# A two-layer decoder trunk on one core: second-half operands formed later, six early units, and a second load queue

## The chip, the cores and the metric

The kernel runs on one core of one Trainium2 chip. The metric is device time in microseconds (us) of one execution, the median of several runs; lower is better. Engines are named as in the profile: PE (TensorE), DVE (VectorE), ACT (ScalarE), POOL (GpSimd) and SP (SyncE, which here issues transfers only; "SPq" is its queue).

## The reference

All is float32, with 1024 tokens and a model width of 1024. The change lies in the last four blocks:

```python
def _short_conv_layer(x, norm_w, in_w, conv_w, out_w):
    h = _rmsnorm(x, norm_w) @ in_w                     # 1024 -> 3 * 1024
    gate_b, gate_c, v = _split(h, (SC_WIDTH, SC_WIDTH, SC_WIDTH))
    y = gate_b * _causal_dwconv(gate_c * v, conv_w)
    return x + y @ out_w

def _swiglu_ffn(x, norm_w, w_gate, w_up, w_down):      # 1024 -> 2816 -> 1024
    h = _rmsnorm(x, norm_w)
    return x + (jax.nn.silu(h @ w_gate) * (h @ w_up)) @ w_down

# layer 0: x = attention and state-space mixer (x); x = _swiglu_ffn(x, ...)
# layer 1: x = _short_conv_layer(x, ...);           x = _swiglu_ffn(x, ...)
# then a last _rmsnorm
```

## The kernel before

The first 900 us (mixer layer) are not touched. From there the work is six matrix stages, each with a right and a left operand of 2 x 2 blocks: ffn0 in, ffn0 out, conv in, conv out, ffn1 in, ffn1 out. Every stage multiplies the blocks with seven products instead of eight (Strassen's scheme in Winograd's form), so sums of blocks are formed as operands. Float32 accuracy comes from a split into a high part (`hi`, a cast on ACT, L169) and a low part (`lo`, a subtraction on DVE, L170), and three matmuls: hi x hi, hi x lo, lo x hi.

An **in stage** (ffn0 in, conv in, ffn1 in) has x as right operand, normalised, as blocks H1 to H7 (`hh`, `hl`), and weights as left operand in units of 256 columns: 22 units for each ffn, 12 for the conv. A unit is seven products of 12 matmuls (`prod`, L1264 to L1266). Its raw weights come by two loads into the tag `wr` (L1215, two buffers), DVE forms four sums of them in place (product 6's step, L1226 to L1228, and product 3's), and each product's weights are split into a buffer `wc` (tag `w`, eight of them). Products 1 and 2 need only H1 and H2, which come from the first half of the tokens; the others need the second half. So the first `EARLY_U` = 4 units run their products 1 and 2 ahead ("early" products), while the second half is normalised, and these units have only five products later.

An **out stage** (ffn0 out, conv out, ffn1 out) runs its seven products one after the other, each over 11 k-steps (ffn) or 4 (conv). A k-step is again 12 matmuls (`step_on`, L1395 to L1397). Its left operand is loaded for two k-steps at once (`lr`, 512 KB, L1378, the same two buffers `wr`), its right operand for each (`rr`, 256 KB, L1380, tag `t` of 42 buffers). ACT and DVE split both into `wc` and `rh`, `rl`. The residual x is loaded from DRAM (L1565, in the last stage L1616), POOL adds an earlier product's result to it ahead of a product's steps (L1411 and L1414), DVE adds each product that comes (L1440), and `spill` (L1455) writes the new x back.

A **border** is the way from an out stage, or the mixer layer, to the next in stage. `norm_first` normalises the first half (L1468), `norm_second` the second: `rsbcast` yields the row factor `rb` (ACT L997, L998), then DVE normalises and forms the sums for H6, H7, H5, H4, H3 and splits all five (20 `lo` subtractions on L170).

`Steps(7)` prepares weights and operands up to seven steps ahead of PE (`self.st.get()`). All code is emitted by hand in this order; a scheduler then sorts the instructions by simulated time, and what comes out is one fixed list for each engine, run in order. Each DMA stands in the list of the engine that issues it, and a DMA that waits for its buffer holds up what stands behind it there. `wsums` (POOL) forms, beside an ffn's in stage, weight sums for the out stage and writes them to DRAM (`wd`, `d_wl`, L1329 and L1339).

Of the kernel before, what the change touches and what calls it, by code (L numbers as in the profile page):

```python
# [9 lines left out]
F32R = mybir.dt.float32r  # L10
# [65 lines left out]
class Steps:  # L76


    def __init__(self, ahead):
        self.ahead, self.fns, self.made, self.pos = ahead, [], [], 0  # L80

    def add(self, fn, test=None):
        self.fns.append((fn, test))

    def get(self):
        while len(self.made) < min(self.pos + self.ahead + 1, len(self.fns)):
            fn, test = self.fns[len(self.made)]
            if test is not None and not test():
                break
            self.made.append(fn())  # L90
        assert self.pos < len(self.made)
        r, self.made[self.pos] = self.made[self.pos], None
        self.pos += 1
        return r


class Trunk:
# [1105 lines left out]

    EARLY_U = 4

    def unit_steps(self, src, prods):

# [24 lines left out]

        for i in prods:
            self.st.add(lambda i=i: step(i))

# [13 lines left out]

    def plan_in(self, srcs):  # L1250

        for src in srcs[:self.EARLY_U]:
            self.early_steps(src)
        for n, src in enumerate(srcs):
            self.unit_steps(src, [i for i in self.UNIT if n >= self.EARLY_U or i not in (1, 2)])

# [112 lines left out]
    def plan_out(self, nk, order, L, R, ready):  # L1369

        nc = self.nc
        st = {}

        def step(i, k):
            if k % 2 == 0:
                n = min(2, nk - k)
                st["l"] = self.wp.tile([P, 2, HF], F32, name=self.uid("lr"), tag="wr", bufs=2)
                nc.sync.dma_start(st["l"][:, :n], L(i, k, n))  # L1378
            r = self.t(nm="rr")
            nc.sync.dma_start(r.rearrange("p (k m) -> p k m", k=1), R(i, k, 1))  # L1380
# [18 lines left out]
    def out_products(self, nk, order, load, done):  # L1399
# [4 lines left out]
        for n, i in enumerate(order):  # L1404
            for ab in {4: ((1, 0),), 2: ((0, 0),), 5: ((1, 1), (0, 1))}.get(i, ()):
                X[ab] = [load(ab, p) for p in range(4)]
            ps = [(self.ps, self.mm)[n % 2]() for _ in range(4)]
            pre = {4: ((1, 0), "u3"), 2: ((0, 0), "p1"), 5: ((1, 1), "u3")}.get(i)
            if pre:
                for p in range(4):  # L1410
                    self.add(X[pre[0]][p], X[pre[0]][p], U[pre[1]][p], nc.gpsimd)  # L1411
            if i == 5:
                for p in range(4):
                    self.add(X[0, 1][p], X[0, 1][p], U["u2"][p], nc.gpsimd)  # L1414
# [55 lines left out]

    def norm_second(self, key, H):

        nc = self.nc
        h0, h1 = self.HO
        x, w = self.x, [self.vt[key][:, k:k + 1] for k in range(KT)]
        rb = self.rsbcast(self.ssq[h1], 1.0 / D, self.last[h1])
        t3, t2 = [], []
        for k in range(4):
            t = self.s(nm="t3")
            nc.scalar.activation(t, x[k][h1], AF.Copy, scale=w[k])  # L1480
            nc.vector.scalar_tensor_tensor(t, x[4 + k][h1], w[4 + k], t, op0=ALU.mult, op1=ALU.subtract)
            t3.append(t)
        for k in range(4):
            nc.vector.tensor_tensor(t3[k], t3[k], rb, op=ALU.mult)
            t2.append(self.s(nm="t2"))
            self.add(t2[k], t3[k], x[k][h0])
            H.setdefault(6, []).append(self.hsplit(t2[k], self.t))
        H[7] = [self.hsplit(t, self.t) for t in t3]
        for k in range(4):
            b = x[k][h1]  # L1490
            nc.vector.scalar_tensor_tensor(b, b, w[k], rb, op0=ALU.mult, op1=ALU.mult)
            self.sub(b, b, x[k][h0])
            H.setdefault(5, []).append(self.hsplit(b, self.t))
        for k in range(4):
            b = x[4 + k][h0]
            self.sub(b, b, t2[k])
            H.setdefault(4, []).append(self.hsplit(b, self.s))
        for k in range(4):
            b = x[4 + k][h1]
            nc.vector.scalar_tensor_tensor(b, b, w[4 + k], rb, op0=ALU.mult, op1=ALU.mult)  # L1500
            H.setdefault(3, []).append(self.hsplit(b, self.s))


    def plan_ffn(self, ly, side):
# [4 lines left out]
        self.plan_in(srcs)  # L1509
        dn = a[ly + "_w_down"]  # L1510
# [50 lines left out]
    def xload(self, d):  # L1561
        def load(ab, p):
            j, hf = ab[0] * 4 + p, self.HO[ab[1]]
            t = self.s(nm="x")
            self.nc.sync.dma_start(t, d[j * P:(j + 1) * P, hf * HF:(hf + 1) * HF])  # L1565
            self.x[j][hf] = t
            return t
        return load

    def out_to_x(self, nk, d_x, d_new, key, H):  # L1570
# [3 lines left out]
        def done(ab, p, x):  # L1574
# [4 lines left out]
            if n[b] == KT:  # L1579
                if d_new is not None:  # L1580
                    self.spill(d_new, hf)
                else:
                    self.turn(hf)
# [18 lines left out]
    def out_final(self, st):  # L1602
# [37 lines left out]

    def plan_conv(self):
# [3 lines left out]
        self.plan_in(srcs)  # L1645
        dn = a["l1_out_w"]
# [12 lines left out]
    def conv_in(self, st, H, second):  # L1659
# [21 lines left out]

        def cb(q):
            def cons(i, j, t):
                o = S[q][1][i, j]
                nc.vector.tensor_tensor(o, t, o, op=ALU.mult)
            return cons
# [15 lines left out]
    def run(self):  # L1702
# [45 lines left out]
        self.st = Steps(7)  # L1748
        f0, cv, f1 = self.plan_ffn("l0", "R"), None, None
        cv = self.plan_conv()  # L1750
        f1 = self.plan_ffn("l1", "L")
        d = [self.dp.tile([D, T], F32, name=f"d_r{i}") for i in range(2)]
        self.d_xT = self.dp.tile([T, D], F32, name="d_xT")
        H = [{} for _ in range(3)]
        h0, h1 = self.HO
# [43 lines left out]
```

## Time and profile before

| | |
|---|---|
| median of 3 runs | 2675.13 us (2670.62 to 2688.19) |
| profiled execution | 2673.26 us, its span 2671.5 us |
| PE busy | 2392.3 us (90%), 10674 matmuls |
| DVE busy | 2029.8 us (76%) |
| ACT busy | 1118.3 us (42%) |
| POOL busy | 637.5 us (24%) |

The execution's own time stands 1.8 us above its span, and 1.9 us below the median. Busy shares are means over stages with different limits, so the rows below go by stretches. The six stages lie, to some 10 us, at: ffn0 in 913 to 1350, ffn0 out 1350 to 1620, conv in 1620 to 1880, conv out 1880 to 1990, ffn1 in 1990 to 2400, ffn1 out 2400 to 2671. Border A is the one into ffn0 in (905 to 945), B the one into conv in (1620 to 1665), C the one into ffn1 in (1985 to 2030).

### The profile page before, as it was taken

How to read it: one execution, taken by the hardware profiler on the slowest of the kernel's cores; microseconds unless marked ns; L12 is line 12 of the kernel's file. 1: busy time of each engine (PE TensorE's matmuls, PEld its weight loads, DVE VectorE, ACT ScalarE, POOL GpSimd, SP SyncE). 2: the span in 40 equal slices, each digit the busy share in tenths (PEclk: the TensorE clock that was granted, in tenths of full speed). 3: DMA queues.
4: the chain of work that ended last, by engine and by line, in shares of the span. 5: the costliest groups of instructions: out<-in, count | busy, mean ns of one | idle time of the engine just before them, and what ended most of it. 6: DMA issues, size and time to landing. Idle time of an engine off the chain costs nothing.

```text
span 2671.5 us, 32103 instructions
## 1 busy us (share of the span) xinstructions
PE 2392.3 (90%) x10674; PEld 1928.7 (72%) x10674; DVE 2029.8 (76%) x3453; ACT 1118.3 (42%) x2092; POOL 637.5 (24%) x562
## 2 busy tenths in 40 slices
PE   6999978778999579999999877999976999999997
PEld 4788766566877468888877655888765888888775
DVE  4799977974687878989965567988778877775655
ACT  4655534544686522332333344323444323334333
POOL 2132236753102355555530010000110000000300
PEclk8999989889999889999999988999988999999998
DMA  4222354445844257666775552233643332336644
GB/s 117 72 79 87 123 172 145 140 128 186 235 133 133 97 193 240 217 218 231 238 255 196 186 180 82 70 117 115 204 161 95 107 111 88 106 111 213 236 159 148
DMA packets 300501, 408.82 MB, mean 153 GB/s; under 512 B 28018, under 2 KB 165424, under 8 KB 300336
## 3 DMA queue, kind: packets, MB, share of 16 engines
q1 hardware_dynamic: 281392, 348.04, 40.9%
q0 software_dynamic: 16640, 54.54, 6.0%
q10 hardware_dynamic: 2304, 4.20, 0.4%
q8 instruction: 84, 1.38, 0.2%
q14 instruction: 81, 0.66, 0.1%
HBM read 286.86 MB, written 117.21 MB: 151 GB/s over the span
## 4 chain that ended last, share of the span: by engine, by line
PE 33%; DVE 13%; DMA 9%; ACT 3%; issue 3%; SPq 1%; DVEq 0%; ACTq 0%
PE mm L1264 5%; PE mm L1265 5%; PE mm L1266 5%; DVE wc L170 4%; DMA rr<-d_gl 4%; PE ps L1264 3%; PE ps L1265 3%; PE ps L1266 3%; PE ps L1396 2%; PE ps L1395 2%; PE ps L1397 2%; DVE u L1191 1%; DMA wr<-in_l_w_gate_dram 1%; PE mm L1396 1%; DVE wr L1194 1%
## 5 line engine op out<-in xcount | busy, mean ns | idle before, releaser
L169 ACT CAST wc<-wr 128x512 fp32r<-128x512 f32 x336 | 203.2, 619 | 567.9 <-DVE wr L1194 289.6
L1264 PE MATMUL mm<-hh,wc 128*128 128x512 f32 x896 | 349.9, 391 | 0.0
L1265 PE MATMUL mm<-hl,wc 128*128 128x512 f32 x896 | 349.8, 391 | 0.0
L1266 PE MATMUL mm<-hh,wc 128*128 128x512 f32 x896 | 348.4, 390 | 0.0
L1264 PE MATMUL ps<-hh,wc 128*128 128x512 f32 x672 | 266.8, 397 | 74.6 <-ACT wc L169 74.5
L1191 POOL TENSOR_TENSOR x<-x,u 128x512 f32<-128x512 f32 x36 | 56.7, 1607 | 1045.7 <-DVE u L1191 553.5
L170 DVE TENSOR_TENSOR wc<-wr,wc 128x512 fp32r<-128x512 f32 x336 | 254.5, 762 | 31.2 <-ACT wc L169 27.2
L1266 PE MATMUL ps<-hh,wc 128*128 128x512 f32 x672 | 265.2, 395 | 6.7 <-DVE wc L170 6.7
L1265 PE MATMUL ps<-hl,wc 128*128 128x512 f32 x672 | 264.4, 393 | 0.0
L170 DVE TENSOR_TENSOR rl<-rr,rh 128x512 fp32r<-128x512 f32 x182 | 136.3, 753 | 137.1 <-ACT rh L169 136.7
L59 POOL TENSOR_TENSOR wl<-wr,wh 128x1024 fp32r<-128x1024 f32 (+1 forms) x55 | 136.1, 2476 | 362.1 <-ACT wh L58 351.8
L160 PE MATMUL mm<-hh,wh 128*128 128x512 f32 (+1 forms) x496 | 198.7, 402 | 11.5 <-ACT hh L301 7.4
L170 DVE TENSOR_TENSOR wc<-lr,wc 128x512 fp32r<-128x512 f32 x182 | 139.1, 767 | 88.5 <-ACT wc L169 88.2
L1264 PEld LDWEIGHTS ps<-hh,wc 128*128 128x128 f32 x672 | 128.0, 191 | 104.5 <-ACT wc L169 77.6
L169 ACT CAST rh<-rr 128x512 fp32r<-128x512 f32 x182 | 112.0, 618 | 213.8 <-DMA rr<-d_gl 114.5
L161 PE MATMUL mm<-hl,wh 128*128 128x512 f32 (+1 forms) x496 | 198.8, 401 | 0.1
L162 PE MATMUL mm<-hh,wl 128*128 128x512 f32 (+1 forms) x496 | 198.3, 400 | 0.0
L1264 PEld LDWEIGHTS mm<-hh,wc 128*128 128x128 f32 x896 | 169.3, 189 | 35.5 <-ACT wc L169 0.2
L1265 PEld LDWEIGHTS mm<-hl,wc 128*128 128x128 f32 x896 | 169.2, 189 | 35.4
L1266 PEld LDWEIGHTS mm<-hh,wc 128*128 128x128 f32 x896 | 168.5, 188 | 35.4 <-DVE wc L170 0.4
L1396 PE MATMUL ps<-rl,wc 128*128 128x512 f32 x416 | 165.0, 397 | 12.6 <-DVE rl L170 12.6
L169 ACT CAST wc<-lr 128x512 fp32r<-128x512 f32 x182 | 112.1, 620 | 148.2 <-PE ps L1397 55.5
(424 smaller groups left out, 5546.2 us busy)
## 6 DMA issues: line engine op xcount, KB each, us to landing
wr<-in_l_in_w_dram SPq DMA_DIRECT2D x54, 512.0 KB
wd<-in_l_w_down_dram POOLq DMA_DIRECT2D x88, 256.0 KB, 4.9
wr<-in_l_w_gate_dram SPq DMA_DIRECT2D x44, 512.0 KB
d_wl<-wd POOLq DMA_DIRECT2D x88, 256.0 KB, 2.8
wr<-in_l_w_up_dram SPq DMA_DIRECT2D x44, 512.0 KB
rr<-d_gl SPq DMA_DIRECT2D x77, 256.0 KB
lr<-d_gl SPq DMA_DIRECT2D x35, 512.0 KB
wr<-in_l_out_w_dram SPq DMA_DIRECT2D x24, 512.0 KB
```

Of the source, the lines that this page charges most:

```text
L59: nc.gpsimd.tensor_tensor(lo, raw, f32(hi), op=ALU.subtract)
L160: self.nc.tensor.matmul(out, ah, bh, start=i == 0, stop=False)
L161: self.nc.tensor.matmul(out, ah, bl, start=False, stop=False)
L162: self.nc.tensor.matmul(out, al, bh, start=False, stop=i == n - 1)
L169: self.nc.scalar.copy(hi, src)
L170: (eng or self.nc.vector).tensor_tensor(lo, src, f32(hi), op=ALU.subtract)
L1191: (eng or self.nc.vector).tensor_tensor(out, a, b, op=ALU.add)
L1264: self.nc.tensor.matmul(ps, wh[:, ks], h, start=k == 0, stop=False)
L1265: self.nc.tensor.matmul(ps, wh[:, ks], l, start=False, stop=False)
L1266: self.nc.tensor.matmul(ps, wl[:, ks], h, start=False, stop=k == n - 1)
L1395: self.nc.tensor.matmul(ps, wh[:, js], h, start=start, stop=False)
L1396: self.nc.tensor.matmul(ps, wh[:, js], l, start=False, stop=False)
```

## The change

Five things are edited. (1) `EARLY_U` is 6. (2) `norm_second` forms only what H6 needs (eight normalisations, four differences, four sums `t2`, four splits); H7, H5, H4 and H3 are formed by functions that `Steps.note` puts between the weight steps of the first unit. The four ACT scalings (L1480) fall away, and DVE's operations are 44 instead of 48. (3) `lr`, the loads of x and the spills are issued from POOL's queue; `rr` and the weight loads of the in stages stay on SP. (4) The 48 additions into x move from POOL to DVE, and from a product's start to the middle of its steps. (5) At border C the second half's transposition (`turn`) is emitted behind `rsbcast`; in conv in, a multiplication is held until its partner is there.

```diff
-    EARLY_U = 4
+    EARLY_U = 6
...
         for i in prods:
+            if i in parts:
+                self.st.note(parts[i])
             self.st.add(lambda i=i: step(i))
...
-                nc.sync.dma_start(st["l"][:, :n], L(i, k, n))
+                nc.gpsimd.dma_start(st["l"][:, :n], L(i, k, n))
             r = self.t(nm="rr")
             nc.sync.dma_start(r.rearrange("p (k m) -> p k m", k=1), R(i, k, 1))
...
-            pre = {4: ((1, 0), "u3"), 2: ((0, 0), "p1"), 5: ((1, 1), "u3")}.get(i)
-            if pre:
-                for p in range(4):
-                    self.add(X[pre[0]][p], X[pre[0]][p], U[pre[1]][p], nc.gpsimd)
...
             for k in range(nk):
                 ops.append(self.st.get())
+                if k == nk // 2:
+                    for ab, u in pre:
+                        for p in range(4):
+                            self.add(X[ab][p], X[ab][p], U[u][p])
...
-            self.nc.sync.dma_start(d[j * P:(j + 1) * P, hf * HF:(hf + 1) * HF], self.x[j][hf])
+            self.nc.gpsimd.dma_start(d[j * P:(j + 1) * P, hf * HF:(hf + 1) * HF], self.x[j][hf])
...
+        self.rb = rb = self.rsbcast(self.ssq[h1], 1.0 / D, self.last[h1])
+        if mid is not None:
+            mid()
+        self.t2 = []
         for k in range(4):
...
+            for j in (k, 4 + k):
+                b = x[j][h1]
+                nc.vector.scalar_tensor_tensor(b, b, self.vt[key][:, j:j + 1], rb, op0=ALU.mult, op1=ALU.mult)
+            self.sub(x[k][h1], x[k][h1], x[k][h0])
+            t = self.s(nm="t2")
+            self.sub(t, x[4 + k][h1], x[k][h1])
+            self.t2.append(t)
+            H.setdefault(6, []).append(self.hsplit(t, self.t))
+
+    def norm_parts(self, H):
...
+        def part(i, js, hf, minus):
+            def f():
+                H[i] = []
+                for k, j in enumerate(js):
+                    b = self.x[j][hf]
+                    if minus is not None:
+                        self.sub(b, *minus(k, b))
+                    hi, lo = self.t(F32R, nm="hh"), self.s(F32R, nm="hl")
+                    self.split(hi, lo, b)
+                    H[i].append((hi, lo))
+            return f
...
-            self.nc.sync.dma_start(t, d[j * P:(j + 1) * P, hf * HF:(hf + 1) * HF])
+            self.nc.gpsimd.dma_start(t, d[j * P:(j + 1) * P, hf * HF:(hf + 1) * HF])
...
-            nc.sync.dma_start(t, self.d_xT[r:r + P, ab[1] * HF:(ab[1] + 1) * HF])
+            nc.gpsimd.dma_start(t, self.d_xT[r:r + P, ab[1] * HF:(ab[1] + 1) * HF])
...
-        self.ffn_in(f1, H[2], lambda: self.norm_second("ffn1", H[2]))
+        self.ffn_in(f1, H[2], lambda: self.norm_second("ffn1", H[2], lambda: self.turn(h1)))
```

DVE at border B, from the first normalisation to the last weight sum of unit 0. Before, these are 51 instructions; `t`, `x` and `sq` are the sums, the residual and `rb`, `hl` the low parts, `s` and `wr` the weight sums, whose last one is the last line:

```order
L1484 TENSOR_TENSOR t_3028_14004<-t_3028_14004,sq_13746 128x512
...
L1491 SCALAR_TENSOR_TENSOR x_13482<-x_13482,c_425,sq_13746 128x512
...
L170 TENSOR_TENSOR hl_14020<-t_3032_14017,hh_14019 128x512
...
L170 TENSOR_TENSOR hl_14121<-x_13480,hh_14120 128x512
L1194 TENSOR_TENSOR s_3084_14150<-wr_14146 128x512
L1191 TENSOR_TENSOR c_3080_14144<-ps_14145,p_3076_14124 128x512
...
L1194 TENSOR_TENSOR wr_14148<-wr_14148,wr_14146 128x4x128
```

The same stretch in the changed kernel, 36 instructions from the first normalisation to the last weight sum (the line with `wr_14143` as output), with some of what follows:

```order
L1492 SCALAR_TENSOR_TENSOR x_13478<-x_13478,c_425,sq_13742 128x512
...
L1201 TENSOR_TENSOR t_3028_14003<-x_13470,x_13478 128x512
...
L177 TENSOR_TENSOR hl_14033<-t_3037_14030,hh_14032 128x512
L1687 TENSOR_TENSOR c_3044_14056<-c_3052_14096,c_3044_14056 128x512
L1201 TENSOR_TENSOR s_3065_14145<-wr_14141 128x512
...
L1201 TENSOR_TENSOR wr_14143<-wr_14143,wr_14141 128x4x128
...
L177 TENSOR_TENSOR hl_14169<-x_13142,hh_14168 128x512
...
L177 TENSOR_TENSOR wc_14149<-wr_14141,wc_14149 128x512
```

The sixteen low parts of H7, H5, H4 and H3 now stand behind the first unit's weight sums, seven of them still ahead of that unit's first low part (`wc_14149`, ten places behind the last sum). At border A the scheduler did not do this: there 55 instructions stand from the first normalisation to the last weight sum, where 52 did; at border C 52, where 52 did.

SP in ffn0 out before, at the place where half of a product's x is spilled and the next is loaded (`d_r` written, `x` read):

```order
L1380 DMA rr_13252<-d_gl_8296 128x512
L1455 DMA d_r_8303<-x_13146 128x512
L1455 DMA d_r_8303<-x_13148 128x512
L1380 DMA rr_13273<-d_gl_8296 128x512
L1455 DMA d_r_8303<-x_13150 128x512
L1455 DMA d_r_8303<-x_13152 128x512
L1565 DMA x_13474<-d_r_8302 128x512
...
L1565 DMA x_13488<-d_r_8302 128x512
L1378 DMA lr_13567<-d_wl_8297 128x512
L1380 DMA rr_13317<-d_gl_8296 128x512
```

POOL at the same place in the changed kernel:

```order
L1389 DMA lr_13378<-d_wl_8297 128x2x512
L1389 DMA lr_13511<-d_wl_8297 128x2x512
L1464 DMA d_r_8303<-x_13142 128x512
...
L1464 DMA d_r_8303<-x_13148 128x512
L1581 DMA x_13470<-d_r_8302 128x512
...
L1581 DMA x_13484<-d_r_8302 128x512
L1389 DMA lr_13555<-d_wl_8297 128x512
L1389 DMA lr_13578<-d_wl_8297 128x2x512
```

The `rr` loads are alone on SP now, and an `lr` load has the four spills and eight loads of x ahead of it on POOL. At the start of ffn0 out the first ten `lr` loads stand on POOL between the last three groups of `wsums`.

## Rows read from the trace of the kernel before

**Rows 1.** What PE waited for, whole span (us in total, times, longest).

```profile
PE ps L1264 <- ACT wc L169: 74.5, 5, 26.3
PE ps L1395 <- ACT rh L169: 23.0, 22, 4.1
PE mm L1395 <- ACT rh L169: 18.6, 15, 2.8
...
PE mm L1396 <- DVE rl L170: 15.0, 6, 9.1
```

**Rows 2.** PE's waits in three stretches: 905 to 1045, 1640 to 1700, 2000 to 2060.

```profile
PE ps L1264 <- ACT wc L169: 29.5, 3, 26.3
...
PE ps L1264 <- ACT wc L169: 19.9, 1, 19.9
...
PE ps L1264 <- ACT wc L169: 25.0, 1, 25.0
```

**Rows 3.** Windows: us, busy PE, PEld, DVE, ACT, POOL, granted clock, DMA share, GB/s.

```profile
1360.00:1600.00 240.00, 202.69 (x835) 157.38 (x834) 140.37 (x198) 94.03 (x165) 35.26 (x29) 0.96 0.59 200
1640.00:1680.00 40.00, 20.07 (x83) 16.17 (x82) 37.37 (x62) 17.41 (x33) 0.00 (x0) 0.74 0.12 34
1700.00:1740.00 40.00, 40.00 (x178) 33.13 (x177) 38.08 (x68) 12.39 (x22) 0.00 (x0) 1.00 0.28 82
1880.00:2000.00 120.00, 102.56 (x455) 80.19 (x453) 89.38 (x122) 59.01 (x103) 25.63 (x16) 0.94 0.54 183
...
2440.00:2520.00 80.00, 80.00 (x355) 66.24 (x354) 45.35 (x68) 36.58 (x65) 3.87 (x3) 1.00 0.62 213
2520.00:2640.00 120.00, 103.90 (x418) 80.43 (x417) 69.19 (x101) 46.35 (x90) 21.91 (x14) 0.94 0.59 195
```

**Rows 4.** Timeline of DVE at border B (start, us, instructions).

```profile
1629.37 2.50 DVE L1484 TENSOR_TENSOR t<-t,sq 128x512 f32<-128x512 f32 x4 [2.92 <-ACT sq L998]
...
1649.13 7.30 DVE L170 TENSOR_TENSOR hl<-x,hh 128x512 fp32r<-128x512 f32 x12
1656.36 0.68 DVE L1194 TENSOR_TENSOR s<-wr 128x512 f32<-128x512 f32 x1
...
1660.07 0.69 DVE L1194 TENSOR_TENSOR wr<-wr,wr 128x512 f32<-128x512 f32 x1
```

**Rows 5.** Timeline of DVE in ffn0 in, where two units' weight sums begin.

```profile
947.73 0.69 DVE L1194 TENSOR_TENSOR s<-wr 128x512 f32<-128x512 f32 x1 [5.10 <-DMA wr<-in_l_w_up_dram]
...
966.83 0.69 DVE L1194 TENSOR_TENSOR s<-wr 128x512 f32<-128x512 f32 x1 [4.76 <-DMA wr<-in_l_w_gate_dram]
```

**Rows 6.** The chain of waits in ffn0 out (start, us, what).

```profile
1522.81 0.37 SPq L1378
1523.22 4.01 DMA rr<-d_gl
1527.26 0.63 ACT rh L169
...
1528.52 0.69 DVE wc L170
1529.23 0.37 SPq L1378
```

**Rows 7.** The chain of waits at the start of ffn0 out and in ffn1 out.

```profile
1337.77 4.01 DMA lr<-in_l_w_down_dram
...
1360.41 6.62 DMA rr<-d_gl
...
2527.18 6.71 DMA lr<-d_gl
```

**Rows 8.** DMA issues of the page (KB each, median us from issue to landing).

```profile
wd<-in_l_w_down_dram POOLq DMA_DIRECT2D x88, 256.0 KB, 4.9
```

**Rows 9.** POOL's groups by line (count, busy us, mean ns, idle before).

```profile
L1191 POOL TENSOR_TENSOR x<-x,u 128x512 f32<-128x512 f32 x36 | 56.7, 1607 | 1045.7 <-DVE u L1191 553.5 <-DMA x<-d_r 414.6 <-DVE wc L170 77.6
...
L1339 POOL DMA_DIRECT2D wd<-in_l_w_down_dram x88 | 47.7, 543 | 98.8 <-DMA d_wl<-wd 64.6 <-ACT sq L1177 15.8 <-issue 15.4
```

**Rows 10.** Timeline of POOL at border A, and of DVE in ffn0 out.

```profile
916.03 17.32 POOL L1191 TENSOR_TENSOR wd<-wd,wd 128x512 f32<-128x512 f32 x1 [2.60 <-DMA wd<-in_l_w_down_dram]
...
1542.51 11.83 DVE L1468 SCALAR_TENSOR_TENSOR x<-x,c,sq 128x512 f32<-128x512 f32 x8 [2.20 <-ACT sq L998]
```

More of the change, by code (lines that the diff above doesn't have):

```diff
@@ L79, in __init__, with note @@
     def __init__(self, ahead):
-        self.ahead, self.fns, self.made, self.pos = ahead, [], [], 0
+        self.ahead, self.fns, self.made, self.pos, self.nxt = ahead, [], [], 0, 0
     def add(self, fn, test=None):
-        self.fns.append((fn, test))
+        self.fns.append((fn, test, True))
+    def note(self, fn):
+        self.fns.append((fn, None, False))
     def get(self):
-        while len(self.made) < min(self.pos + self.ahead + 1, len(self.fns)):
-            fn, test = self.fns[len(self.made)]
+        while len(self.made) < self.pos + self.ahead + 1 and self.nxt < len(self.fns):
+            fn, test, real = self.fns[self.nxt]
             if test is not None and not test():
                 break
-            self.made.append(fn())
+            self.nxt += 1
+            r = fn()
+            if real:
+                self.made.append(r)
         assert self.pos < len(self.made)
@@ L1202, in wsplit, with unit_steps @@
         return hi, lo
-    EARLY_U = 4
-    def unit_steps(self, src, prods):
+    EARLY_U = 6
+    def unit_steps(self, src, prods, parts):
         nc = self.nc
@@ L1248, with plan_in @@
     UNIT = (1, 6, 7, 5, 2, 4, 3)
-    def plan_in(self, srcs):
+    def plan_in(self, srcs, parts):
         for src in srcs[:self.EARLY_U]:
@@ L1254, in plan_in @@
         for n, src in enumerate(srcs):
-            self.unit_steps(src, [i for i in self.UNIT if n >= self.EARLY_U or i not in (1, 2)])
+            self.unit_steps(src, [i for i in self.UNIT if n >= self.EARLY_U or i not in (1, 2)],
+                            parts if n == 0 else {})
     def prod(self, H, i):
@@ L1407, in out_products @@
             ps = [(self.ps, self.mm)[n % 2]() for _ in range(4)]
-            pre = {4: ((1, 0), "u3"), 2: ((0, 0), "p1"), 5: ((1, 1), "u3")}.get(i)
-            if pre:
-                for p in range(4):
-                    self.add(X[pre[0]][p], X[pre[0]][p], U[pre[1]][p], nc.gpsimd)
-            if i == 5:
-                for p in range(4):
-                    self.add(X[0, 1][p], X[0, 1][p], U["u2"][p], nc.gpsimd)
+            pre = {4: (((1, 0), "u3"),), 2: (((0, 0), "p1"),), 5: (((1, 1), "u3"), ((0, 1), "u2"))}.get(i, ())
             ops = []
@@ L1469, in norm_first, with norm_second @@
             H.setdefault(1 + k // 4, []).append(self.hsplit(x, self.t))
-    def norm_second(self, key, H):
+    def norm_second(self, key, H, mid=None):
         nc = self.nc
         h0, h1 = self.HO
-        x, w = self.x, [self.vt[key][:, k:k + 1] for k in range(KT)]
-        rb = self.rsbcast(self.ssq[h1], 1.0 / D, self.last[h1])
-        t3, t2 = [], []
-        for k in range(4):
[L1479 to L1501, printed above, removed]
@@ L1504, in plan_ffn @@
-    def plan_ffn(self, ly, side):
+        x = self.x
+        self.rb = rb = self.rsbcast(self.ssq[h1], 1.0 / D, self.last[h1])
+        if mid is not None:
+            mid()
+        self.t2 = []
+        for k in range(4):
+            for j in (k, 4 + k):
[6 more added lines that the diff above has]
+            H.setdefault(6, []).append(self.hsplit(t, self.t))
@@ new lines, in norm_parts @@
+    def norm_parts(self, H):
+        h0, h1 = self.HO
+        def part(i, js, hf, minus):
[9 more added lines that the diff above has]
+            return f
+        lo, up = range(4), range(4, KT)
+        return {7: part(7, lo, h0, lambda k, b: (self.t2[k], b)), 5: part(5, lo, h1, None),
+                4: part(4, up, h0, lambda k, b: (b, self.t2[k])), 3: part(3, up, h1, None)}
@@ L1506, in plan_ffn @@
+    def plan_ffn(self, ly, side, H):
         a = self.a
@@ L1508, in plan_ffn @@
         srcs = [a[f"{ly}_w_{w}"][:, p * 256:(p + 1) * 256] for p in range(NP) for w in ("gate", "up")]
-        self.plan_in(srcs)
+        self.plan_in(srcs, self.norm_parts(H))
         dn = a[ly + "_w_down"]
@@ L1581, in done @@
                     self.spill(d_new, hf)
-                else:
+                elif b == 0:
                     self.turn(hf)
@@ L1638, in out_final, with plan_conv @@
         self.out_products(st["NP"], self.SEVEN["L"], load, done)
-    def plan_conv(self):
+    def plan_conv(self, H):
         a = self.a
@@ L1644, in plan_conv @@
         srcs = [a["l1_in_w"][:, col[w] + q * 256:col[w] + (q + 1) * 256] for w, q in self.CVB]
-        self.plan_in(srcs)
+        self.plan_in(srcs, self.norm_parts(H))
         dn = a["l1_out_w"]
@@ L1682, in cb @@
         def cb(q):
+            held = []
             def cons(i, j, t):
-                o = S[q][1][i, j]
-                nc.vector.tensor_tensor(o, t, o, op=ALU.mult)
+                held.append((i, j, t))
+                acc = S[q][1]
+                while len(acc) == 4 and held:
+                    i, j, t = held.pop()
+                    nc.vector.tensor_tensor(acc[i, j], t, acc[i, j], op=ALU.mult)
             return cons
@@ L1748, in run @@
         self.st = Steps(7)
-        f0, cv, f1 = self.plan_ffn("l0", "R"), None, None
-        cv = self.plan_conv()
-        f1 = self.plan_ffn("l1", "L")
+        H = [{} for _ in range(3)]
+        f0, cv, f1 = self.plan_ffn("l0", "R", H[0]), self.plan_conv(H[1]), self.plan_ffn("l1", "L", H[2])
         d = [self.dp.tile([D, T], F32, name=f"d_r{i}") for i in range(2)]
         self.d_xT = self.dp.tile([T, D], F32, name="d_xT")
-        H = [{} for _ in range(3)]
         h0, h1 = self.HO
```

## The prediction

> **What bounds the kernel now.** I read first what PE waited for, then windows at the places named there, then the timeline of the engine that it waited for, then the chain of waits. PE at the full clock does 178 matmuls in 40 us (1700 to 1740) [rows 3], 0.225 us each, so a product of 12 takes 2.7 us. In the second half it falls short of that at two kinds of places.
>
> *Borders.* The longest waits are for the high part of the first unit's weights: 26.3 (of 29.5 us), 19.9 and 25.0 us [rows 1, 2]. That cast is cheap; it waits for the weight sums, and these stand behind the whole of `norm_second` in DVE's list. At border B DVE goes without a pause from the first normalisation at 1629.37, through 12 of the low parts at 1649.13, to the sums, which begin at 1656.36 and end at 1660.76 [rows 4]: 31.4 us for 51 instructions, 0.61 us each. The window 1640 to 1680 holds 83 matmuls of 178, at a clock of 0.74 of the higher level [rows 3]: 95 x 0.225 = 21 us lost, 1.5 more than the wait.
>
> *Out stages.* There the waits are short and many, for `rh` and `rl` [rows 1]. By windows: ffn0 out, 1360 to 1600, 835 matmuls of 1068, 52 us lost; conv out, 1880 to 2000, 455 of 534, 18 us; ffn1 out, 2520 to 2640, 418 of 534, 26 us, while 2440 to 2520 was full with 355 of 356 [rows 3]. So 96 us lie there. The chain shows the mechanism: `lr` is issued at 1522.81, `rr` behind it at 1523.22, that lands after 4.01 us, ACT casts it, DVE ends the next weights' low part, and only this frees the buffer for the next `lr` at 1529.23 [rows 6]. That is 6.42 us for two k-steps which PE does in 5.4: `rr`, which has buffers to spare, is held behind `lr`, which has two. What starts it are transfers on the same queue (spills and x), the burst of DVE's normalisation, 11.83 us for eight instructions [rows 10], and, at the stage's start, loads that take 6.6 us instead of 4 [rows 7].
>
> **The change part by part.** Sums are against the profiled execution of 2673.3 us, which lies 1.9 us under the median.
>
> *Border B.* To the last weight sum 36 instructions instead of 51, at 0.61 us: 22 us, so about 1651.5 instead of 1660.8. The early products end 4 products, 10.9 us, later than 1641.4 (1661.3 less 19.9), at 1652. The first high part is then just in time, but its low part has ten more instructions ahead (6 us), so PE stalls about 5 us: 15 of 19.9 us gained. Against it stand the 16 low parts that DVE now does in the stage itself, where it is busy 38 of 40 us [rows 3]: if none of them finds a gap, 9.8 us come back. I take 15, bounds 5 to 20.
>
> *Border C.* 52 instructions to the sums as before, so the first unit's weights are no earlier by that. PE has four more early products, 10.9 us. `rb` no longer waits for four ACT scalings, but the in-place normalisation waits for the transposition, which I count as 1. I take 12, bounds 6 to 16.
>
> *Border A.* 55 instructions instead of 52, 1.8 us later, against 10.9 us more of early products: 9 us less wait. But here units 4 and 5 lose products 1 and 2 later. One unit's weight buffers turn in 19.1 us in this stage (947.73 to 966.83, each time waiting for the load) [rows 5]; seven products, 18.9 us, hide that, five, 13.5, don't, so each of the two loses 5.5 us. I take 0, bounds -5 to 9. In conv in and ffn1 in PE ran full after the border [rows 3], so there I don't charge this.
>
> *Out stages.* Three edits act together. `rr` is alone on SP and can run ahead to the limit of its 42 buffers: the loop of 6.42 us is cut. The 48 additions leave POOL (1.607 us each [rows 9]) and cost DVE 48 x 0.61 = 29 us, in stages where it is busy 140 of 240 us [rows 3], so nearly all is hidden; and the eight normalisations, which ran beside POOL's additions, should come from 1.5 us to about 0.7 each, the rate of border B. What remains: a burst of DVE still delays `rl`, the start of ffn0 out still has slow loads, and `lr` now stands behind spills and x loads on POOL, 12 issues of 0.543 us [rows 9], 6.5 us, at such a place. Recovered I take about half: 28 of 52 in ffn0 out (bounds 8 to 42), 7 of 18 in conv out (0 to 12), 12 of 26 in ffn1 out (0 to 22), where 15 x loads stand between two `lr`. The upper bounds leave the normalisation bursts and the slow start, the lower ones the case in which POOL's queue stands where SP's stood.
>
> Whether `lr` on POOL is quick enough decides this. Two buffers and 5.4 us for a pair leave 10.8 us for one turn; of it 2.7 pass between the pair's two weights, 0.63 and 0.69 in ACT and DVE [rows 6], 0.54 in the issue [rows 9]. So the load may take 6.2 us. On SP a 512 KB load took 4.01 us, and 6.71 in the burst of x loads [rows 7]; POOL's loads of half that size took 4.9 [rows 8]. No row shows 512 KB from POOL; between 4.0 and 7.5 I take 5.5, nearer to the 4.9, since those were sent in fours.
>
> A rule of the Trainium skill speaks against the move. The rows first: POOL issued 88 `wd` loads at 543 ns each [rows 9], many beside a busy DVE, and yet one POOL addition took 17.32 us while DVE worked without a pause [rows 10]. "SBUF — State Buffer", section "SBUF: two separate sides", says that descriptors of transfers issued from POOL are written by GpSimd, which DVE can shut out of the port they share, and advises SP's or ACT's queue. The mean of the issues disagrees with it here, the 17.32 us agree with the port. By the page the out stages' gain would shrink; the rival for it is below, from rows.
>
> Sum: 0 + 15 + 12 + 28 + 7 + 12 = 74 us; 2673.3 - 74 = 2599 for a profiled execution, 2601 for the median.
>
> **The rivals.** *Out stages give nothing* (about 2648): POOL's queue takes the part that SP's had, with `lr` behind `wsums` at the start of ffn0 out, behind spills that wait for DVE, behind x. For it: the 6.5 us of issues at each such place are just what a load may take. Against: `rr` is free of it, and 2440 to 2520 was full even with both on one queue. Only the borders' 27 us stay.
>
> *Borders give nothing* (about 2628): DVE does the deferred work in a stage where it is busy 95% of the time, and the shorter border comes back as waits in the first units. Only the 47 us of the out stages stay. For it: 38.08 of 40 us [rows 3]. Against: 16 instructions are 10 us, and the four more early products cover as much.
>
> *Slower* (about 2700): the landing time of `lr` from POOL lies above its 6.2 us. A pair is then late by the excess each time, and there are about 35 pairs and 7 single loads in each ffn's out stage and 14 pairs in conv out, 98 loads. Those 98 times the excess take the place of the 96 us lost now: at 7.2 us only the borders' gain remains, from about 7.5 us the kernel is slower, and at 7.7 it loses 147 - 96 - 27 = 24 us. For it: 6.71 us even on SP under load.
>
> *POOL shut out by DVE* (about 2635): issues of `lr` are delayed until DVE's bursts end. With six bursts in each ffn's out stage (two normalisations of half an x, four groups of additions) of 5 us less the slack of some 2, 12 x 3 = 36 us of the 74 are given back.
>
> **How the numbers follow.** Forecast 0.50; out stages give nothing 0.22; borders give nothing 0.12; slower 0.12; shut out 0.04. The bounds of the six terms, taken as independent, spread the forecast by about 25 us to either side, 2576 to 2626. The range goes from 2565 to 2662: it takes in most of the borders-only case, and leaves out the slower one and the ends. A run of this kernel can tell 1%, 27 us, from no change: faster than 2648 are the forecast, borders-nothing, shut-out, and half of out-stages-nothing, less a little, 0.74; within 1% 0.14, slower 0.12.
>
> **What would show it.** Border B: PE's wait before the first unit falls from 19.9 to some 5 us, and is for DVE's low part. Border C: from 25 to some 13; border A: from 26 to some 17, with as many microseconds more lost by 1045 as in rows 3's manner can be counted. Out stages: SP's queue waits for PE or DVE's `rl`, not for `wc`; windows there rise towards 178 for 40 us; the eight normalisations take under 6 us. POOL's queue should show `lr` landing within 6 us. The forecast is wrong if `lr` becomes what ACT's `wc` waits for in most pairs, or if conv in after border B holds under 170 matmuls in 40 us.

## The result and the profile after

The changed kernel takes 2605.37 us (median of 4 runs, 2598.16 to 2616.67), the kernel before 2681.66 us over the runs that now stand beside it (6.5 us more than in the first three); the ratio is 0.9711 with a 95% interval of 0.9639 to 0.9784. The profiled execution has a span of 2599.0 us against 2671.5, 72.5 us less. The forecast was 74 us less, and 2601 with a range of 2565 to 2662.

PE's waits in the changed kernel (us in total, times, longest), whole span, then the second half's stretches 905 to 1060, 1375 to 1600, 1590 to 1700, 1835 to 1960, 1955 to 2060 and 2370 to 2599; they answer to [rows 1, 2]:

```profile
PE ps L1275 <- ACT wc L176: 36.7, 10, 9.6
...
PE ps L1275 <- ACT wc L176: 18.7, 5, 9.6
PE ps L1277 <- DVE wc L177: 5.5, 2, 5.0
PE mm L1275 <- ACT wc L176: 5.1, 1, 5.1
...
PE mm L1407 <- DVE rl L177: 4.8, 3, 3.6
PE ps L1407 <- DVE rl L177: 2.3, 2, 1.7
...
PE ps L1275 <- ACT wc L176: 6.5, 2, 5.9
...
PE ps L996 <- DVE sq L1198: 7.7, 1, 7.7
...
PE ps L1275 <- ACT wc L176: 4.6, 1, 4.6
...
PE ps L1407 <- DVE rl L177: 0.4, 1, 0.4
```

The three long waits for the first unit's weights at the borders (26.3, 19.9 and 25.0 us) are 9.6, 5.9 and 4.6 us at the longest; at border C a wait of 7.7 us for DVE's squares is new. The waits for ACT's `rh`, 41.6 us in [rows 1], are gone from the top of the list; ffn1 out waits 0.4 us for `rl` where the same view of before adds up to 16.1 for `rh` and `rl`. Windows (us, busy PE, PEld, DVE, ACT, POOL, granted clock, DMA share, GB/s), to [rows 3]:

```profile
900.00:1060.00 160.00, 127.37 (x508) 100.38 (x507) 131.50 (x172) 50.81 (x90) 83.03 (x95) 0.89 0.58 190
1375.00:1595.00 220.00, 212.42 (x915) 171.58 (x914) 141.53 (x222) 98.57 (x174) 51.55 (x80) 0.99 0.68 227
1680.00:1720.00 40.00, 39.65 (x173) 32.03 (x173) 37.42 (x67) 11.63 (x20) 0.00 (x0) 1.00 0.33 98
1840.00:1960.00 120.00, 104.92 (x459) 83.12 (x458) 87.50 (x142) 61.21 (x109) 15.05 (x25) 0.93 0.62 208
2380.00:2580.00 200.00, 199.64 (x880) 164.81 (x879) 120.79 (x199) 89.81 (x172) 33.29 (x52) 1.00 0.64 217
```

ffn0 out does 915 of 979 matmuls, ffn1 out 880 of 890. The window of conv out holds 459 of 534, where it held 455, but part of border C now lies in it: from its first to its last matmul conv out takes 104.2 us, where it took 112.5.

For a sum by stages I read from PE's timeline where each stage's first matmul starts. Five stretches result, here for all profiled kernels, in us. "Lead" is counted in ACT's list: by how many steps the cast of the weights (`wc`) stands ahead of that of the right operand (`rh`), a mean over ffn0 out and over ffn1 out; it becomes important below.

| kernel | up to ffn0 in | ffn0 in | ffn0 out, border B, conv in | conv out, border C, ffn1 in | ffn1 out | lead |
|---|---|---|---|---|---|---|
| before | 890.1 | 467.0 | 512.4 | 555.0 | 247.0 | 4.9, 3.5 |
| changed | 898.8 | 473.8 | 466.9 | 537.1 | 222.4 | 4.3, 1.6 |
| e1_early4 | 892.9 | 467.3 | 477.4 | 545.6 | 223.2 | 3.6, 1.6 |
| e2_lr_sp | 896.8 | 475.8 | 497.5 | 542.5 | 242.8 | 4.9, 3.4 |
| e3_x_sp | 889.8 | 485.9 | 482.5 | 536.2 | 232.2 | 4.3, 2.8 |
| e4_pool_adds | 894.3 | 473.5 | 485.7 | 549.6 | 223.1 | 4.4, 0.1 |
| e5_queues | 899.2 | 471.7 | 490.0 | 555.1 | 225.4 | 3.8, 0.1 |
| e6_adds | 893.2 | 473.7 | 505.0 | 549.0 | 240.9 | 5.0, 3.5 |
| e7_norm | 891.9 | 484.7 | 498.3 | 552.4 | 244.2 | 5.0, 3.5 |
| e9_ffn0_4 | 891.4 | 468.9 | 467.7 | 537.6 | 222.0 | 3.6, 1.6 |
| e10_both | 891.9 | 474.8 | 464.3 | 535.9 | 222.0 | 3.6, 1.6 |
| e11_swap | 889.3 | 469.6 | 515.3 | 543.8 | 251.6 | 5.5, 5.2 |
| e12_late | 897.0 | 476.6 | 475.0 | 540.4 | 226.6 | 3.0, 1.7 |
| e13_lists | 877.1 | 489.4 | 479.1 | 543.8 | 230.4 | 2.2, 1.1 |

From before to changed: +8.7, +6.8, -45.5, -17.9, -24.6, in sum -72.5.

These stretches put a border together with an out stage. To part them I take PE's time lost: a part's time, less 0.227 us for each of its matmuls (the spacing in PE's timeline where it runs full). An out stage goes from its first to its last matmul, and a border counts to the in stage behind it.

| part | lost before | lost, changed | gain | forecast (bounds) |
|---|---|---|---|---|
| ffn0 in: border A and the first six units | 47.3 | 45.8 | 1.5 | 0 (-5 to 9) |
| ffn0 in: the other sixteen units | 0.7 | 9.1 | -8.4 | none |
| ffn0 out | 51.5 | 13.0 | 38.5 | 28 (8 to 42) |
| border B and conv in | 22.0 | 14.9 | 7.1 | 15 (5 to 20) |
| conv out | 19.9 | 9.3 | 10.6 | 7 (0 to 12) |
| border C and ffn1 in | 24.6 | 17.3 | 7.3 | 12 (6 to 16) |
| ffn1 out | 25.7 | 0.8 | 24.9 | 12 (0 to 22) |

With the 8.7 us lost ahead of ffn0 in, the out stages gave 74 us and everything else together about nothing.

### The profile page after: what moved, and what is told of

Read it like the earlier page. It is cut to its first block, busy times and chain, and to the rows that moved or that the text cites. A ratio compares the mean times of both kernels' runs of the same rounds, so it can differ in the third digit from the quotient of the medians.

```text
span 2599.0 us, 32096 instructions
## 1 busy us (share of the span) xinstructions
PE 2393.8 (92%) x10674; PEld 1935.4 (74%) x10674; DVE 2012.3 (77%) x3489; ACT 1105.2 (43%) x2080; POOL 664.0 (26%) x692
## 4 chain that ended last, share of the span: by engine, by line
PE 39%; DVE 13%; DMA 7%; issue 5%; ACT 2%; POOL 1%; SPq 0%; DVEq 0%; POOLq 0%; ACTq 0%
PE mm L1275 5%; PE mm L1277 5%; PE mm L1276 5%; PE ps L1277 4%; PE ps L1275 4%; PE ps L1276 4%; DVE wc L177 3%; PE ps L1407 3%; PE ps L1408 2%; PE ps L1406 2%; DMA wr<-in_l_w_up_dram 2%; DMA wr<-in_l_w_gate_dram 2%; PE mm L1407 2%; PE mm L1408 2%; PE mm L1406 2%
## 5 line engine op out<-in xcount | busy, mean ns | idle before, releaser
L1275 PE MATMUL mm<-hh,wc 128*128 128x512 f32 x896 | 353.3, 394 | 11.7 <-ACT wc L176 6.7
L177 DVE TENSOR_TENSOR wc<-wr,wc 128x512 fp32r<-128x512 f32 x336 | 246.3, 739 | 44.9 <-ACT wc L176 42.1
L177 DVE TENSOR_TENSOR wc<-lr,wc 128x512 fp32r<-128x512 f32 x182 | 128.0, 706 | 120.7 <-ACT wc L176 120.5
L1389 POOL DMA_DIRECT2D lr<-d_gl x42 | 28.9, 687 | 610.6 <-DVE wr L1201 444.7
L1408 PE MATMUL ps<-rh,wc 128*128 128x512 f32 x416 | 162.6, 392 | 0.0
L177 DVE TENSOR_TENSOR rl<-rr,rh 128x512 fp32r<-128x512 f32 x182 | 126.2, 695 | 41.0 <-ACT rh L176 41.0
```

The source lines that it names most:

```text
L177: (eng or self.nc.vector).tensor_tensor(lo, src, f32(hi), op=ALU.subtract)
L1275: self.nc.tensor.matmul(ps, wh[:, ks], h, start=k == 0, stop=False)
L1408: self.nc.tensor.matmul(ps, wl[:, js], h, start=False, stop=stop)
```

## The experiments

**One part undone at a time.** `e1_early4` sets `EARLY_U = 4` again.

> The changed kernel with four early units instead of six. My theory: the early products pay at the borders into conv in and ffn1 in (up to 10.9 us each) and not at the one into ffn0 in, where two more units of five products wait for weight loads. Then the stretch from the first out step of ffn0 to the first of conv out gets 5 to 10 us longer than 467 us, the one from there to the first of ffn1 out some 10 longer than 537, ffn0 in some 7 shorter than 474; in all 10 to 15 us slower than the changed kernel (2610 to 2620). Rival: ffn0 in lost for another reason (its order of DVE work), so that it stays near 474 or gets longer by up to 11, and the whole is 25 to 30 us slower.

Ratio 0.9696 (0.9662 to 0.9730), span 2606.4. The stretches look as the first theory said: ffn0 in 6.5 us shorter, the next two 10.5 and 8.5 longer. By time lost they say less. Of the 10.5, 7.3 lie in ffn0 out, 6.0 of them in one wait for an addition of DVE's at its start; border B and conv in lose 3.3 more than with six early units, border C and ffn1 in 7.4. In ffn0 in, border A and the first six units lose 43.9 us with four early units and 45.8 with six, so most of the 6.5 doesn't lie where the theory put it. The part ahead of ffn0 in came out 5.9 shorter, and the runs' times don't tell six units everywhere from four.

`e2_lr_sp`:

```diff
-                nc.gpsimd.dma_start(st["l"][:, :n], L(i, k, n))
+                nc.sync.dma_start(st["l"][:, :n], L(i, k, n))
```

> The changed kernel with lr back on SP's queue, ahead of rr as before; spills and x stay on POOL's queue, the additions on DVE. My theory: lr that waits for its two buffers holds rr behind it, and this loop made the out stages slow; then 30 us or more of the out stages' gain go, most in ffn0 out and ffn1 out, with PE waiting for ACT's rh again (2630 to 2650). Rival 1: the spills and x on that queue started the loop, and without them it doesn't start: within 10 us of 2602. Rival 2: POOL's additions were the cause: within 10 us as well, but then the run with the additions back on POOL loses the 30.

Ratio 0.9894 (0.9863 to 0.9924): some 49 us of the 77 are gone. The first out stretch is 30.6 us longer and ffn1 out 20.4, and PE's waits for `rh` are back (19.1 us in ffn0 out, 11.0 in ffn1 out; 0.2 and none in the changed kernel). Where `lr` is issued carries most of the out stages' gain. ACT's waits in ffn0 out for the load of `rr` (us in total, times, longest), in the kernel before, the changed one and `e2_lr_sp`:

```profile
ACT rh L169 <- DMA rr<-d_gl: 103.2, 40, 10.4
...
ACT rh L176 <- DMA rr<-d_gl: 16.5, 7, 4.8
...
ACT rh L176 <- DMA rr<-d_gl: 83.1, 34, 6.7
```

`e3_x_sp` puts the spills and both loads of x back on SP (three lines, `gpsimd` to `sync`).

> The changed kernel with the spills and the x loads back on SP's queue, beside rr; lr stays on POOL. My theory (lr ahead of rr is what costs): rr can run ahead of a burst of x loads by its buffers, so at most 10 us of the out stages go (2602 to 2612), and the first border, whose spills left POOL, gets up to 8 us back. Rival (the bursts on SP are what costs): 20 to 30 us slower, with waits for rh right behind the x loads.

Ratio 0.9790 (0.9757 to 0.9824), some 21 us slower than the changed kernel: 15.6 and 9.8 us in the two ffn out stretches. My theory allowed 10; the bursts do matter. (Ffn0 in is 12.1 us longer; every variant has other lists there.)

`e4_pool_adds` puts the 48 additions back to POOL, at a product's start.

> The changed kernel with the 48 additions back on POOL at a product's start; the queues stay as changed. POOL now also issues lr, so an addition that waits for x holds lr behind it. My theory: with the additions on POOL the eight normalisations slow down again to about 1.5 us each (6 us in each out stage but the last) and lr waits behind eight additions of 1.6 us at three places: 20 to 35 us slower than the changed kernel (2620 to 2640). Rival: the additions don't matter, within 8 us.

Ratio 0.9770 (0.9733 to 0.9806): some 16 us slower by the ratio, 27 by the profiled executions, so between the theory and its rival. In the profiles 18.8 lie in the first and 12.5 in the second out stretch, none in ffn1 out. The normalisation of x in the kernel before and in this run, by line (duration min/median/max in ns):

```profile
L1468 DVE SCALAR_TENSOR_TENSOR x<-x,c,sq x24: 737/942/1833, 867.5 to 1956.4; 128x512 f32<-128x512 f32 x24
...
L1476 DVE SCALAR_TENSOR_TENSOR x<-x,c,sq x24: 736/739/8154, 871.3 to 1947.2; 128x512 f32<-128x512 f32 x24
```

In the kernel before, six of the eight in ffn0 out took 1744 to 1764 ns, in turn with POOL's additions of 1.7 us, evenly as I had read from 11.83 us [rows 10]. Here one took 8154 ns, and six of POOL's additions ran back to back inside it (7.38 us in all from 1542.04); the changed kernel's longest takes 752. Where the two met, one waited for the other, in turn or for six together.

**One part alone, on the kernel before.** `e5_queues` only moves `lr`, x and spills to POOL, `e6_adds` only the additions, `e7_norm` is only the reordered `norm_second` with `norm_parts` (and the held multiplication).

> The kernel before with only the queues changed: lr, the x loads and the spills on POOL, the additions still on POOL, the borders as they were. Putting lr alone back on SP cost some 49 us, so my theory says that the queues alone carry most of the out stages' gain: 35 to 55 us faster than before, less the 10 to 20 us that lr loses behind POOL's additions, so a ratio of 0.98 to 0.99; the borders' waits stay at 20 to 26 us. Rival: the parts need each other (lr on POOL is worth nothing while POOL also adds): within 1% of before.

> The kernel before with only the 48 additions moved to DVE, in the middle of a product's steps. My theory: the queue is what costs, so this gives under 10 us, mostly from the eight normalisations going from 11.8 to about 5.4 us in ffn0 out. Rival (the additions on POOL slow the out stages by themselves): 20 us or more, a ratio under 0.993.

> The kernel before with only the reordered forming of the right operands (and the multiplication held in conv in); four early units, queues, additions and the transposition as before. By the order the border into conv in has 15 DVE instructions fewer ahead of the first weight sums: my theory is 5 to 12 us faster, all of it in the stretch from the first out step of ffn0 to the first of conv out. Rival: the moved low parts return in the unit that follows: no change, within 4 us.

Ratios 0.9812 (0.9777 to 0.9847), 0.9879 (0.9840 to 0.9918) and 0.9898 (0.9854 to 0.9942). The queues give 22.4 us in the first out stretch and 21.6 in ffn1 out; the additions 7.4, 6.0 and 6.1; the reordering 14.1 in the stretch with border B. But by time lost only 3.4 of these 14.1 lie at border B and in conv in, and 10.7 in ffn0 out, where no edit of `e7_norm` stands but the lists are others: PE's wait at border B fell from 19.9 to 15.3 us by the reordering, and only with six early units to 5.9. In the first out stretch the three come to 43.9 us of 45.5, to which the early products' 10.5 would have to be added, so they overlap. The queues came out as expected (50 us). The additions, 32 us by the runs' times and 19.5 by the three stretches, fit the rival rather than my under 10: on POOL they cost by themselves. The reordering gave less than the 5 to 12 us of its theory at the border, and 27 by the runs' times; its profiled execution was 17.7 us longer in ffn0 in. (The kernel before was profiled in an execution of 2673.26 us, where its later runs' medians are 2686 to 2691, so sums against that profile come out smaller than the ratios.)

**Four early units in ffn0 only.** `e9_ffn0_4` gives `plan_in` and `early` a number for each stage; `e10_both` also issues the two spills of border A from SP.

> The changed kernel with four early units in ffn0 in only, six in conv in and ffn1 in. If ffn0 in loses 7 us by its two more units of five products, and the others gain, this is 5 to 10 us faster than the changed kernel (ratio about 0.968). Rival: the run with four units everywhere came out at the same time as six because all three borders gain nothing; then this does too, within 4 us.

> The changed kernel with four early units in ffn0 in, six in the other in stages, and the spills of the first border issued from SP. The run with four units there had a ratio of 0.967 to before; over the runs with profiles the time up to ffn0 in's first matmul was 890 to 893 us with these spills on SP and 891 to 899 with them on POOL. If POOL's spills cost there, this is 3 to 5 us faster than that run (a ratio of 0.965 to 0.967); rival: that spread is between runs, and it comes out within 2 us of it.

`e9_ffn0_4`: 0.9673 (0.9623 to 0.9722). `e10_both`: median 2589.66 us of 6 runs, 0.9636 (0.9610 to 0.9661), the best of all kernels here; its interval overlaps that of the changed kernel, which was timed beside other runs. Its span, 2588.9, is 10.1 us shorter, of which 6.9 lie ahead of ffn0 in. Over the runs that part is 889.3 to 893.2 us with the spills on SP (six kernels, mean 891.0) and 891.4 to 899.2 with them on POOL (seven, mean 895.8; `e13_lists` aside, which has other buffers there). Against `e9_ffn0_4`, the run that it was to beat, the part is no shorter (891.9 and 891.4) and the intervals overlap, as the rival said. PE's waits are clearer. Between 800 and 850 us, where the first spills are issued, PE waits for DVE's row maxima (`mx`), in `e9_ffn0_4` and in `e10_both`:

```profile
PE mm L1069 <- DVE mx L1072: 4.2, 2, 2.5
...
PE mm L1069 <- DVE mx L1072: 0.7, 1, 0.7
```

It is 3.5 to 5.5 us in the seven kernels with the spills on POOL and 0.6 to 0.7 in the six with them on SP. So the spills on POOL do cost some 3 to 5 us there; between these two runs a difference of 3.9 us that arose earlier in the mixer hid it. Ffn0 in with four units took 467 to 475 us under the changed lists, with six 470 to 486, so its few us are not settled by single profiles.

**Queue or list?** `e11_swap` exchanges the queues: `rr` on POOL, and `lr`, x and spills on SP.

> The changed kernel with the queues exchanged: rr on POOL, and lr, the x loads and the spills on SP. My theory is that what helps is that rr, which has buffers to run ahead, no longer stands behind lr, whichever engine issues which; then the out stages hold within some 10 us of the changed kernel, 2600 to 2615. Rival: POOL's queue or SP's has a part of its own in it (rr behind the last weight sums on POOL, or x and spills ahead of lr on a queue where issues are quicker): then more than 20 us differ, and the start of ffn0 out or ffn1 out shows which.

Ratio 0.9948 (0.9925 to 0.9972): nearly everything in the out stages is lost, though `rr` stands behind no `lr`. My theory fell. ACT's timeline (start, us) in ffn0 out shows how, first in the changed kernel:

```profile
1478.72 0.62 ACT L176 CAST wc<-lr 128x512 fp32r<-128x512 f32 x1 [0.63 <-PE mm L1408]
1479.24 0.61 ACT L176 CAST rh<-rr 128x512 fp32r<-128x512 f32 x1
1481.44 0.62 ACT L176 CAST wc<-lr 128x512 fp32r<-128x512 f32 x1 [1.58 <-PE mm L1408]
```

and in `e11_swap`, with PE at the same time:

```profile
1473.69 0.63 ACT L176 CAST wc<-lr 128x512 fp32r<-128x512 f32 x1 [1.58 <-PE ps L1408]
1477.64 0.62 ACT L176 CAST wc<-lr 128x512 fp32r<-128x512 f32 x1 [3.33 <-PE mm L1408]
1478.17 1.13 ACT L176 CAST rh<-rr 128x512 fp32r<-128x512 f32 x2
...
1478.83 1.19 PE L1406 MATMUL mm<-rh,wc 128*128 128x512 f32 x4 [1.23 <-ACT rh L176]
```

No `rh` waits for its load here, nor anywhere in ffn0 out. ACT waits 3.33 us for PE to free a weight buffer (eight of them), casts weights for a step far ahead, and only then the two `rh`, the first of which PE has been waiting for. The order on ACT is fixed beforehand, and by the lead in the table the weights' cast stands 5.5 and 5.2 steps ahead here. The farther it runs ahead, the closer to PE's own step the `rh` behind it is. DVE's list has the same form, and in ffn0 out PE waits longer for its `rl` (22.1 us) than for ACT's `rh` (17.1). Over the fourteen kernels ffn1 out follows the lead: 222 to 227 us up to 1.7 (230.4 in `e13_lists`), 232.2 at 2.8, 241 to 247 at 3.4 to 3.5, 251.6 at 5.2. Ffn0 out doesn't follow it alone: at a lead of 4.3 to 4.4 the changed kernel loses 13.0 us there, `e3_x_sp` 27.9 and `e4_pool_adds` 32.6, and `e13_lists` loses 24.7 at 2.2. The scheduler sets it by its own times for the loads, so the edit of a queue wrote another list for ACT.

`e13_lists` tests that: `e2_lr_sp` (so `lr` is on SP, ahead of `rr`), with other numbers of buffers, by which the scheduler puts `rh` earlier.

```diff
-        w = self.wp.tile([P, 2, HF], F32R, name=self.uid("wc"), tag="w", bufs=8)
+        w = self.wp.tile([P, 2, HF], F32R, name=self.uid("wc"), tag="w", bufs=7)
...
-        self.scope(t=42)
+        self.scope(t=44)
```

The first half's two tiles of that tag go to 7 as well.

> The run with lr back on SP (ahead of rr, as in the kernel before), with one weight buffer w fewer (7 instead of 8) and two more buffers t (44 instead of 42). By this the scheduler writes other lists: on ACT the weights' cast of a step stands 2 and 1 steps on average ahead of the right operand's cast in ffn0 out and ffn1 out, where it stood 5 and 3 steps ahead with lr on SP, 4 and 2 in the changed kernel and 5 steps in both with the queues exchanged. Theory of the lists: a weights' cast waits for PE to free its buffer, and the right operand's cast behind it on ACT comes too late when it is for a step close to the one that PE is in; the farther the weights run ahead, the worse. Then this run holds the out stages near the changed kernel (467 and 222 us for the two stretches, within 12) although lr is on SP, near 2610. Theory of the queues: lr that waits on SP holds rr behind it, whatever the lists; then it stays near the run with lr on SP, 497 and 243 us, near 2655. One weight buffer fewer can cost some us in each in stage and in the mixer by itself.

Ratio 0.9780 (0.9732 to 0.9828). The first out stretch is 18.4 us shorter than with the old lists (of the 30.6 that lie between `e2_lr_sp` and the changed kernel), ffn1 out 12.4 (of 20.4), while SP's queue still waits for the weights' split ahead of `lr`, 142.0 us here and 157.4 in `e2_lr_sp`:

```profile
SPq L1389 <- DVE wc L177: 142.0, 38, 7.3
```

So other lists bring back some 60% without moving `lr`. The two further buffers `t` hardly did it by themselves: in `e2_lr_sp` the `rr` loads waited for PE to free one for 6 us in all of ffn0 out. `rh` still waits for its load as before,

```profile
ACT rh L176 <- DMA rr<-d_gl: 87.6, 34, 6.0
```

but PE's waits for `rh` there fell from 19.1 to 9.8 us. The rest, 12 and 8 us, can be the queue itself, with its late loads, or the buffer less; that stays open. The whole run's time doesn't decide between the theories: the mixer's part is 21.7 us shorter than in the changed kernel and ffn0 in 15.6 longer.

**Slack of `lr`.** `e12_late`:

```diff
+                nc.gpsimd.memset(st["l"][:, :n], 0.0)
                 nc.gpsimd.dma_start(st["l"][:, :n], L(i, k, n))
```

> The changed kernel with POOL clearing the lr buffer ahead of each lr load, so that each of the 98 loads is sent later by the time of one memset of 128 x 1024 (some 1 to 2.5 us). In the changed kernel lr landed 4.4 to 4.8 us after its issue; the prediction allowed 6.2. My theory: up to a delay of about 1.5 us nothing is lost, under 10 us in all, and beyond that about 90 times the excess, so 0 to 10 us for a memset of 1 to 1.5 us, some 90 for one of 2.5. Rival: there is no such slack, and each pair comes later by the whole memset, 100 us or more.

The memset took 0.893 us (POOL by line, count, busy us, mean ns, idle before):

```profile
L1389 POOL MEMSET lr<- 128x1024 f32 x98 | 87.5, 893 | 939.3 <-DVE wr L1201 683.3 <-DVE wc L177 255.9
```

Ratio 0.9747 (0.9719 to 0.9776), and the three stretches with out stages are 8.1, 3.3 and 4.2 us longer, 15.6 for 87.5 us of delay (some 10 by the ratios): at or above the 10 I allowed, but most of it is hidden. A rival without slack would have lost all of it.

## Why the prediction was right, and where not

*The sum was right by luck, 74 against 72.5 us.* The out stages gave 27 us more than forecast (74 against 47), borders B and C 13 less (14 against 27), and 15.5 were lost up to the end of ffn0 in, where the forecast had 0. The terms:

*Ffn0 out*, 28 with bounds 8 to 42: 38.5. *Border B*, 15 with bounds 5 to 20: 7.1. Together they hide it, 43 against the 45.5 of the stretch. The sums were done earlier as counted, but PE's last 5.9 us of wait there are not for DVE's low part. ACT's timeline at that place:

```profile
1626.14 6.86 ACT L176 CAST hh<-x 128x512 fp32r<-128x512 f32 x13 [1.19 <-DVE x L1201]
...
1634.00 0.61 ACT L176 CAST wc<-wr 128x512 fp32r<-128x512 f32 x1
```

Thirteen `hh` casts for H7 to H3 now stand ahead of the first weights' cast; ACT, not DVE, ends last. The low part costs 1.0 us. Behind the wait PE ran 10 us at the lower of its two clock levels, 18 matmuls where the full clock does 44; the working had no term for that:

```profile
1635.00:1645.00 10.00, 8.76 (x18) 5.84 (x19) 9.96 (x18) 2.26 (x6) 0.00 (x0) 0.50 0.16 45
```

The rival that the borders give nothing had the wrong mechanism: conv in lost 5 matmuls of 178 after the border, and was otherwise full, so the deferred work didn't come back there. In size the borders lie between it and the forecast: A, B and C gave 16 us of 27.

*Conv out*, 7: 10.6. *Border C*, 12: 7.3. The wait before the first unit fell from 25.0 to 4.6, more than forecast, but a wait without a term took its place: PE sits 7.7 us in the matmul of `rsbcast` (L996) until DVE has summed the squares, since in its list the transposition and the early products stand behind it. Then DVE's first normalisation waits 6.4 us for the transposition, which the working counted at 1. The early products give 7.4 at border C (`e1_early4`), the additions 6 to 12 in conv out.

*Border A*, 0 with bounds -5 to 9: ffn0 in is 6.8 us longer, but not at the border. There the early products lost 15.9 us where they had lost 27.6, 11.7 less (forecast 9), and the first six units 29.9 where they had lost 19.7, 10.2 more (charged 11): the term was right. What failed is that nothing was put behind it. PE lost 9.1 us in two later units, with these waits between 1070 and 1372, where the kernel before has none:

```profile
PE ps L1275 <- ACT wc L176: 6.8, 2, 4.6
```

The longer of them, 4.6 us at 1202, comes in the same unit of `e5_queues` (3.0) and `e6_adds` (4.9), which have four early units and the old borders, so the two further early units don't explain it; its cause stays open. Another 8.7 us lie ahead of ffn0 in. The first border's spills, which moved to POOL too, had no term, and cost some 3 to 5 of them (`e10_both`).

*Ffn1 out*, 12 with bounds 0 to 22: 24.9, all of the loss there. In all three out stages half was too little: 74 of 97 us came back.

*The mechanism of the out stages* was right in part only. The loop in [rows 6], with `rr` held behind `lr`, is really there, and taking `lr` off the queue ends it: ACT's waits for `rr` went from 103.2 to 16.5 us in ffn0 out, and SP's queue waits for PE or for DVE's `rl`, which frees `t`,

```profile
SPq L1391 <- PE mm L1408: 56.4, 22, 4.0
SPq L1391 <- DVE rl L177: 54.1, 16, 18.1
```

as the prediction said it would. But separate queues are not enough (`e11_swap`), and some 60% of what `lr`'s queue gave comes with `lr` on SP too, once `rh` stands earlier on ACT (`e13_lists`). The prediction looked at the lists of SP, POOL and DVE, and not at ACT's, where it would have seen the lead, and in [rows 3] a sign of it: 2440 to 2520 was full already with the old queues, where the weights ran mostly 2 to 3 steps ahead, and it broke down where they ran 6. That sign alone proves nothing, since the loads of x start at the same place, from 2517.

*Slower* is out: `lr` landed in good time. DMA issues in ffn0 out, 1380 to 1560 (KB, median us from issue to landing):

```profile
lr<-d_wl POOLq DMA_DIRECT2D x19, 512.0 KB, 4.4
lr<-in_l_w_down_dram POOLq DMA_DIRECT2D x10, 512.0 KB, 4.3
x<-d_r POOLq DMA_DIRECT2D x16, 256.0 KB, 6.2
```

That is below the 5.5 us I took and the 6.2 allowed. Of all 98 loads 21 took longer than 6.2, up to 8.2, and `lr` was what ACT's `wc` waited for in 14 cases in ffn0 out and 13 in ffn1 out, not in most pairs. *POOL shut out* is out for the same reason: all 98 issues of `lr` took 537 to 729 ns, beside a DVE that was busy 142 of 220 us. The rule of the Trainium skill ("SBUF — State Buffer", "SBUF: two separate sides") that DVE, in its 2-port modes, keeps GpSimd from writing descriptors cost nothing that these runs show, and none shows whether DVE ran in such a mode; its other half, that the one which comes second waits for the other's whole instruction, is what the 8154 ns in `e4_pool_adds` look like, though six POOL instructions fit into them.

## What to carry to other kernels

Where a scheduler sorts by simulated time, moving a transfer to another queue also rewrites the lists of engines that it doesn't touch; compare those of every engine between the loads and the bottleneck, and look at what stands behind an instruction that waits for the bottleneck itself. An operand that is needed soon shouldn't stand behind one that is prepared far ahead and waits for a buffer. At a border, work laid ahead of the wait only pays where the stage behind has room to give it back: six early units paid in two stages and not in the one where weight loads set the pace. And a sum that comes out can hide terms that don't: count the loss stage by stage before calling a forecast right.

## What was not expected of the hardware

DVE can stand still for long beside POOL: a DVE instruction of 0.74 us took 8.15 and, in `e5_queues`, 9.18 us beside POOL's additions. A memset of half a megabyte on POOL takes 0.89 us. And with seven weight buffers instead of eight the mixer layer's part was 877.1 us in `e13_lists`, 12 to 22 us shorter than in all other kernels, and ffn0 in with 489.4 the longest of all, in one profile; why was not tried.
